# A decoder layer on one core: the input projection written out as one stream in TensorE's program order

## The chip, the cores and the metric

The kernel runs on one core of a Trainium2 chip. The metric is the device time of one execution in microseconds (us); the median of several executions counts. Beside the times there is one profiled execution, whose trace gives the start and the length of the instructions on each engine: PE (TensorE's matmuls), PEld (its weight loads), DVE (VectorE), ACT (ScalarE), POOL (GpSimd) and SP (SyncE, which issues most DMAs).

## What is computed

One layer (DEPTH is 1) over 2048 rows of 1024 numbers, all float32:

```python
h = rms_norm(x, mix_norm_pre)
z = h @ w_in                                   # 1024 -> 2560: q, k, v, xr, gr of 512 each
attn = dilated_attention(q, k, v)              # 8 heads of 64, three dilation patterns
xr = causal_depthwise_conv(xr, conv_w, conv_b) # four taps
rec = rg_lru(xr, ...) * gelu(gr)               # gates r and i, a linear recurrence over time
x = x + rms_norm(concat([attn, rec]) @ w_out, mix_norm_post)
x = x + rms_norm(squared_relu_mlp(rms_norm(x, mlp_norm_pre)), mlp_norm_post)
```

The gates are `sigmoid(xr @ w_r + b_r)` and `sigmoid(xr @ w_i + b_i)` in blocks of 64; the recurrence is `h[t] = a[t] * h[t-1] + u[t]` with `a = exp(-8 r softplus(-lambda))`.

## The kernel before

Every float32 product is made of three matmuls on a high and a low part of each operand, split with a cast on ACT and a subtraction on DVE or POOL. The sequence is worked in two halves of 1024 rows, each of two blocks `b` of 512 rows. For each half there come the input projection, the attention, the recurrent part, the output projection and the MLP. The attention of the second half is already mixed into the MLP of the first.

This study is about the first stage, which holds the input projection of both halves, the recurrent part of both halves and the attention of the first half. `w_in` is cut into 20 column tiles `ct` of 128: 0 to 3 are q, 4 to 7 k, 8 to 11 v, 12 to 15 xr, 16 to 19 gr. `Project.product` makes one tile for one block: 8 steps over `k` of three matmuls of 512 columns, 24 matmuls, into one PSUM bank named `z`. Two halves, two blocks and 20 tiles make 80 products. `load_w` loads a tile's weights and splits them (`wraw`, `wH`, `wL`); `load_x` loads a block of x transposed and splits it (`hH`, `hL`); `spread_norm` spreads the norm's factors over the partitions through a product with ones (`pbc`, `bc`).

`qkv(hf, pr)` makes q, k and v for a pair of heads and stores them in DRAM. `recurrent_block(hf, c, b)` makes an xr product, the four taps (`xc`, the first on POOL, three on DVE), the two gate matmuls `pr` and `pi`, some ten steps on ACT and DVE up to the scan, the gr product, the gelu (`ge`, its polynomial on POOL) and the output. `attention` has for each head two parts of kind A (scores `S`) and four of kind B (`SB`); each part has its scores, a mask and maximum on DVE, an exponential on ACT (`sm`), transposes on PE (`pT`), a split (`thA`, `tlA` or `thB`, `tlB`) and value products (`oA`, `oB`). `join` merges the two kinds.

The stage is called in the order of the strings `ORDER`, `BETWEEN` and `LATER` (q for `qkv`, r for `recurrent`, a for the attention of a pair, x for `load_x`), but the instructions do not stand in that order: a scheduler of the framework orders every engine's instructions of this stage. From the output projection on, PE's order is that of the code, and in the second half's attention ACT's, DVE's and SP's too: there `interleave` puts the attention's steps between steps of the MLP's second product.

## Time and profile before

| | us |
|---|---|
| median of 3 executions | 2320.88 (2314.49 to 2322.9) |
| profiled execution, its own time | 2311.64 |
| its span in the trace | 2309.9 |
| PE busy | 2184.8 (95%) |
| DVE busy | 1539.9 (67%) |
| ACT busy | 1231.3 (53%) |
| POOL busy | 465.9 (20%) |

The span is the time from the first to the last instruction; a little time lies around it. Matmuls are pipelined, so a PE that is shown busy may still run below its pace: how fast it runs is read from the distance between the starts of equal matmuls. The first matmul of the output projection (`m`) starts at 650.8 us; what lies before is the stage of the change.

### The profile page before, as it was taken

How to read it: one execution, taken by the hardware profiler on the slowest of the kernel's cores; microseconds unless marked ns; L12 is line 12 of the kernel's file. 1: busy time of each engine (PE TensorE's matmuls, PEld its weight loads, DVE VectorE, ACT ScalarE, POOL GpSimd, SP SyncE). 2: the span in 40 equal slices, each digit the busy share in tenths (PEclk: the TensorE clock that was granted, in tenths of full speed). 3: DMA queues.
4: the chain of work that ended last, by engine and by line, in shares of the span. 5: the costliest groups of instructions: out<-in, count | busy, mean ns of one | idle time of the engine just before them, and what ended most of it. 6: DMA issues, size and time to landing. Idle time of an engine off the chain costs nothing.

```text
span 2309.9 us, 30833 instructions
## 1 busy us (share of the span) xinstructions
PE 2184.8 (95%) x10264; PEld 1776.1 (77%) x10264; DVE 1539.9 (67%) x3060; ACT 1231.3 (53%) x2489; POOL 465.9 (20%) x549
## 2 busy tenths in 40 slices
PE   8989989889999899998999999889999999999998
PEld 6668778667788677786777787667878888788887
DVE  6757575887548877674667677767775656545556
ACT  7646464645334555453656666745454545563542
POOL 5543514563213201011001011113200000000003
PEclk9999999999999999999999999999999999999999
DMA  8364574645754586867777777768454433576665
GB/s 288 99 194 154 166 232 146 180 144 151 255 166 155 195 306 255 302 232 268 248 201 211 220 227 204 220 189 257 147 194 169 164 137 155 208 271 195 192 192 182
DMA packets 217553, 466.16 MB, mean 202 GB/s; under 512 B 22465, under 2 KB 77153, under 8 KB 211121
## 3 DMA queue, kind: packets, MB, share of 16 engines
q1 hardware_dynamic: 188624, 329.52, 45.7%
q0 software_dynamic: 28768, 134.66, 16.5%
q8 instruction: 81, 1.33, 0.2%
q14 instruction: 80, 0.65, 0.1%
HBM read 329.75 MB, written 151.13 MB: 208 GB/s over the span
## 4 chain that ended last, share of the span: by engine, by line
PE 59%; DVE 14%; DMA 9%; ACT 7%; issue 5%; POOL 1%; SPq 0%; DVEq 0%; ACTq 0%; POOLq 0%
PE o L1141 6%; PE o L1140 6%; PE o L1142 6%; PE za L1001 4%; PE za L1002 4%; PE za L1003 4%; PE z L198 3%; PE z L199 3%; PE z L200 3%; PE m L827 2%; PE m L825 2%; PE m L826 2%; PE zc L1001 2%; PE zc L1002 2%; PE zc L1003 2%
## 5 line engine op out<-in xcount | busy, mean ns | idle before, releaser
L198 PE MATMUL z<-hH,wH 128*128 128x512 f32 x640 | 263.6, 412 | 17.6 <-ACT wH L54 7.9
L199 PE MATMUL z<-hL,wH 128*128 128x512 f32 x640 | 259.1, 405 | 0.5 <-DVE hL L173 0.5
L200 PE MATMUL z<-hH,wL 128*128 128x512 f32 x640 | 257.9, 404 | 0.0
L198 PEld LDWEIGHTS z<-hH,wH 128*128 128x128 f32 x640 | 122.6, 192 | 51.2 <-ACT wH L54 8.8
L199 PEld LDWEIGHTS z<-hL,wH 128*128 128x128 f32 x640 | 122.3, 191 | 32.0 <-issue 5.1
L200 PEld LDWEIGHTS z<-hH,wL 128*128 128x128 f32 x640 | 122.5, 191 | 28.5 <-issue 3.4
L415 ACT ACTIVATE smB<-smB,negB 128x128 f32<-128x128 f32 (+3 forms) x128 | 71.4, 559 | 103.0 <-DVE negB L411 102.7
L55 POOL TENSOR_TENSOR wL<-wraw,wH 128x512 fp32r<-128x512 f32 x58 | 84.2, 1464 | 115.7 <-ACT wH L54 109.0
L1006 ACT ACTIVATE sq<-sq 128x512 f32<-128x512 f32 x93 | 58.8, 632 | 84.9 <-DVE sq L1010 84.9
L1066 POOL DMA_DIRECT2D sa<-sq x31 | 16.5, 533 | 402.4 <-ACT sq L1007 401.8
L415 ACT ACTIVATE sm<-sm,neg 128x256 f32<-128x256 f32 (+1 forms) x128 | 63.1, 494 | 55.7 <-DVE neg L411 55.2
L55 DVE TENSOR_TENSOR tlB<-pT_B,thB 128x384 fp32r<-128x384 f32 x96 | 57.4, 598 | 44.2 <-ACT thB L54 41.0
L1007 ACT ACTIVATE sq<-sq 128x512 f32<-128x512 f32 x124 | 76.6, 629 | 2.2
L54 ACT CAST wH<-wraw 128x512 fp32r<-128x512 f32 (+1 forms) x81 | 47.2, 612 | 49.5 <-PE z L199 31.7
L1174 POOL TENSOR_TENSOR y<-y,g4b 128x512 f32<-128x512 f32 x8 | 13.0, 1655 | 261.3 <-ACT junk_y L84 261.3
L1077 DVE TENSOR_TENSOR w2s<-w2s 128x512 f32<-128x512 f32 x64 | 44.1, 689 | 32.1 <-DMA w2s<-in_dram 31.2
L404 DVE CUSTOM_DVE_ANT_0 smB<-SB,mask_b 128x128 f32<-128x128 f32 (+3 forms) x128 | 59.5, 482 | 6.8 <-PE pT_B L377 4.2
L377 PE MATMUL pT_B<-ident,smB 128*128 128x128 f32 x320 | 52.7, 280 | 5.3 <-DVE nb L398 2.2
L54 ACT CAST thB<-pT_B 128x384 fp32r<-128x384 f32 x96 | 48.4, 506 | 16.3 <-PE oB L612 14.2
L55 DVE TENSOR_TENSOR tlA<-pT,thA 128x512 fp32r<-128x512 f32 (+1 forms) x64 | 42.5, 668 | 21.0 <-ACT thA L54 20.7
L1001 PE MATMUL za<-hHT,f_6H 128*128 128x512 f32 x128 | 50.6, 396 | 5.2 <-ACT sq L1040 5.1
L1002 PE MATMUL za<-hLT,f_5H 128*128 128x512 f32 x128 | 51.0, 399 | 4.4 <-DVE hLT L55 4.4
(568 smaller groups left out, 7105.7 us busy)
## 6 DMA issues: line engine op xcount, KB each, us to landing
sa<-as POOLq DMA_DIRECT2D x32, 1024.0 KB, 6.5
w1r<-in_dram SPq DMA_DIRECT2D x58, 512.0 KB, 3.8
sa<-sq POOLq DMA_DIRECT2D x31, 768.0 KB, 3.9
wraw<-in_dram SPq DMA_DIRECT2D x79, 256.0 KB, 3.5
w2s<-in_dram SPq DMA_DIRECT2D x16, 1024.0 KB, 7.5
sb<-w2s POOLq DMA_DIRECT2D x16, 1024.0 KB, 6.2
kh<-sk SPq DMA_DIRECT2D x24, 512.0 KB, 5.2
kl<-sk SPq DMA_DIRECT2D x24, 512.0 KB, 6.8
```

What stands on the lines that cost most here:

```text
L54: return (nc.scalar.copy(out=hi, in_=src), (lo_eng or nc.vector).tensor_tensor(out=lo, in0=src, in1=f32(hi), op=ALU.subtract))
L55: (lo_eng or nc.vector).tensor_tensor(out=lo, in0=src, in1=f32(hi), op=ALU.subtract))
L198: pe.matmul(z, hi[:, k, :], hh, start=(k == 0), stop=False)
L199: pe.matmul(z, hi[:, k, :], hl, start=False, stop=False)
L200: pe.matmul(z, lo[:, k, :], hh, start=False, stop=(k == KT - 1))
L415: s.activation(out=sm[:, c0:c0 + w], in_=sm[:, c0:c0 + w], func=AF.Exp, bias=neg[:, j:j + 1], accum_out=st[:, 1, u, cols[j]:cols[j] + 1])
L1001: pe.matmul(o, hi[:, k], bh[:, k], start=start and k == 0, stop=False, skip_group_check=True)
L1002: pe.matmul(o, hi[:, k], bl[:, k], start=False, stop=False, skip_group_check=True)
L1003: pe.matmul(o, lo[:, k], bh[:, k], start=False, stop=k == KH - 1, skip_group_check=True)
L1140: pe.matmul(o, ah[:, ts], bh, start=fresh and j == 0, stop=False, skip_group_check=True)
L1141: pe.matmul(o, ah[:, ts], bl, start=False, stop=False, skip_group_check=True)
L1142: pe.matmul(o, al[:, ts], bh, start=False, stop=j == NJ - 1, skip_group_check=True)
```

## The change

The stage keeps its arithmetic but gets a new frame. `product` becomes a generator that pauses after each of its 8 steps. `stream` runs all products in the order of the table `JOBS` (a token such as `0k3v3` is half 0 and the tiles k3 and v3 together, block by block), loads the weights of the next tile at each tile's first block, and does what follows a product: `stored` (q, k, v), `convolved` and `opened` (taps and gates), `gated` (gelu). What of that needs PE is put off by `after(n, ...)`: it is issued when n further steps of products have gone by. `begin` does the same by hand for the first eight products. PE's instructions of the whole stage are now in program order (`manual_schedule`); those of the other engines are still ordered by the scheduler. The first half's attention goes through `interleave`, which already served the second half's, with gaps of its own, and `join`'s last steps are spread too.

Three pieces of work change engine. The first tap goes from POOL to ACT, and so do from DVE the two small copies of the taps' tail and the square of `r`. The gelu's polynomial, three steps on POOL, becomes a square on ACT and one step on DVE. The copies of `w_out` and `w2` from DRAM to DRAM, which are issued on POOL's queue, came one with each call (`w_out`) and then eight with each call of `recurrent` for the second half (`w2`); now one or two come with each product, from the first stored q on.

```diff
+            if px:
+                made(j)
+                spread(j)
+            else:
+                self.after(4 + 3 * j, lambda j=j: made(j))
+                self.after(6 + 3 * j, lambda j=j: spread(j))
         self.bc[tb % NBH] = bcast
...
     def product(self, hf, ct, w, b, tag="P"):
+
         hi, lo = w
         pe = self.nc.tensor
         z = self.bank(tag, f"z{hf}_{ct}_{b}")
...
-        return z
-
-    def qkv(self, hf, pr):
+            yield z
+
+    def stored(self, kind, hf, pr, b, z):
...
+
+        self.after(4, turned)
...
+    def after(self, n, fn):
+
+        self.due.append([n, fn])
+
+    def passed(self):
+        for d in self.due:
+            d[0] -= 1
+        now = [d for d in self.due if d[0] <= 0]
+        self.due = [d for d in self.due if d[0] > 0]
+        for _, fn in now:
+            fn()
+
+    def stream(self, jobs, between):
+
+
+        first = {"q": 0, "k": 4, "v": 8, "x": 12, "g": 16}
+        jobs = [(int(t[0]), [(t[i], int(t[i + 1])) for i in range(1, len(t), 2)]) for t in jobs.split()]
+        tiles = [(hf, kind, i) for hf, ts in jobs for kind, i in ts]
+        loaded = {}
+
+        def load():
+            if tiles:
+                hf, kind, i = tiles.pop(0)
+                loaded[hf, kind, i] = self.load_w(hf, first[kind] + i)
+
+        load()
+        for hf, ts in jobs:
+            for b in range(NBH):
+                for kind, i in ts:
+                    if b == 0:
+                        load()
+                    between(hf, kind, i, b)
+                    for n, last in enumerate(self.product(hf, first[kind] + i, loaded[hf, kind, i], b)):
+                        self.passed()
+                        if n < KT - 1:
+                            yield
+                    if kind in "qkv":
+                        self.stored(kind, hf, i, b, last)
+                    elif kind == "x":
+                        self.convolved(hf, i, b, last, 10)
+                    else:
+                        self.gated(hf, i, b, last)
+                    yield
+        while self.due:
+            self.passed()
...
+    def begin(self, w, px):
...
+        for c in range(2):
+            product("x", c, 0, "B")
+            product("g", c, 0, "T")
+        self.after(5, first)
+        product("x", 0, 1, "P")
+        product("g", 0, 1, "P")
+        self.after(3, second)
+        product("x", 1, 1, "B")
+        self.gated(0, 0, 1, z["g", 0, 1], px)
+        product("g", 1, 1, "T")
+        followed(1, 1, 24)
+
...
-def interleave(units, rest):
+def interleave(units, rest, begin, gaps, pause=0):
...
-        turn[0]()
-        fill(2)
-        fill(2, ahead[0]())
-        if early:
-            loads[0](False)
-            if k % n == 3:
-                loads.pop(0)
-        turn[1]()
-        fill(2)
-        fill(1 if k + n >= len(todo) else 2 - k % 2, ahead[1]())
+
+        whole = k + 1 < len(todo) and len(todo[k + 1][1]) == 1
+        if pause:
+            then = ahead[0]()
+            fill(gaps[0], ahead[1]() if whole else then)
+            turn[0]()
+            fill(gaps[1])
+            if early:
+                loads[0](False)
+                if k % n == 3:
+                    loads.pop(0)
+            then = None if whole else ahead[1]()
+            fill(gaps[2], then)
+            if len(turn) > 1:
+                turn[1]()
+        else:
+            turn[0]()
+            fill(gaps[0])
+            fill(gaps[1], ahead[0]())
+            if early:
+                loads[0](False)
+                if k % n == 3:
+                    loads.pop(0)
+            turn[1]()
+            fill(gaps[2])
+        fill(gaps[3 + k % 2] if k + n < len(todo) else gaps[5], None if pause else ahead[1]())
         values()
         if ending:
             ends.append(ending())
+            fill(pause)
     while ends:
         fill(1)
 
...
+            def between(hf, kind, i, b):
+
+                if (hf, kind, i, b) in NEWX:
+                    n = NEWX[hf, kind, i, b]
+                    pj.load_x(n)
+                    pj.spread_norm(n)
+                if "pool" not in cst:
+                    return
+                with tc.issue_after(cst["pool"].ins):
+                    for dst, src in copies[:1 if len(copies) > 2 * NJ else 2]:
+                        nc.gpsimd.dma_start(out=dst, in_=src)
+                del copies[:1 if len(copies) > 2 * NJ else 2]
...
-            with sb("at0", "right") as pa:
-                attend = attention(tc, pa, lambda k, n: bank(place[k][0], n), cst, scr, 0, mask_a, mask_b, pa)
-                run(ORDER)
-            pg = per.enter_context(sb("g2", "right"))
-            sh = Shared(pg, bank)
-            run(BETWEEN)
-            lst.close()
-            wo = load_wo(0)
-            pj.lo = nc.vector
-            run(LATER)
+            with tc.manual_schedule(engines={mybir.EngineType.PE}):
+                steps = pj.stream(JOBS, between)
+                for _ in range(8 * AHEADJOBS):
+                    next(steps)
+                xst.close()
+                with sb("at0", "right") as pa:
+                    interleave(attention(tc, pa, lambda k, n: bank(place[k][0], n), cst, scr, 0, mask_a, mask_b, pa), steps,
+                               16, (1, 1, 1, 3, 4, 3), 10)
+                for _ in range(REST):
+                    next(steps)
+                pg = per.enter_context(sb("g2", "right"))
+                sh = Shared(pg, bank)
+                lst.close()
+                wo = load_wo(0)
+                pj.lo = nc.vector
+                for _ in steps:
+                    pass
...
-ORDER = "q00 r02 q01 a0 r03 q02 a1 q03 x2 x3 a2 q10 a3"
-BETWEEN = "r10 r11 r12 r13"
-LATER = "q11 q12 q13"
+
+
+JOBS = ("0q0 0k0 0v0 0x2 0g2 0q1 0k1 0v1 0q2 0k2 0v2 0x3 0q3 0g3 0k3v3 1x0q0 1g0 1k0 1x1 1v0 1g1 1x2 1g2 1x3 1g3 "
+        "1q1 1k1 1v1 1q2 1k2 1v2 1q3 1k3 1v3")
+
+NEWX = {(0, "k", 3, 1): 2, (1, "x", 0, 0): 3}
+AHEADJOBS = 10
+REST = 0
```

The taps, gates and gelu are now these:

```diff
         xr = p.tile([P, TB + 3], F32, tag="xr", bufs=1, name=f"xr{n}")
-        v.tensor_copy(out=xr[:, 0:3], in_=self.tail[:, c, :])
+        s.copy(out=xr[:, 0:3], in_=self.tail[:, c, :])
         v.tensor_tensor(out=in_time(xr[:, 3:TB + 3]), in0=by_residue(zx), in1=by_residue(self.bc[b]), op=ALU.mult)
-        v.tensor_copy(out=self.tail[:, c, :], in_=xr[:, TB:TB + 3])
+        s.copy(out=self.tail[:, c, :], in_=xr[:, TB:TB + 3])
         xc = p.tile([P, TB], F32, tag="xc", bufs=2 if p is self.pl else 1, name=f"xc{n}")
-        self.cst["pool"] = g.tensor_scalar(out=xc, in0=xr[:, 3:TB + 3], scalar1=self.cw[:, c, 3:4],
-                                           scalar2=vec["cb"][:, c:c + 1], op0=ALU.mult, op1=ALU.add)
+        s.activation(out=xc, in_=xr[:, 3:TB + 3], func=AF.Identity, scale=self.cw[:, c, 3:4],
+                     bias=self.vec["cb"][:, c:c + 1])
...
+        self.xc[c, b], self.open[hf, c, b] = xc, None
+        self.after(wait, lambda: self.opened(hf, c, b, p, px))
+
+    def opened(self, hf, c, b, p, px):
...
         pr = self.bank("X", f"pr{n}")
         pe.matmul(pr, self.bd["r"][:, c, :], xc, start=True, stop=True)
-        pi = self.bank("O" if px else "X", f"pi{n}")
-        pe.matmul(pi, self.bd["i"][:, c, :], xc, start=True, stop=True)
...
-        a2 = p.tile([P, TB], F32, tag="la", bufs=1, name=f"a2{n}")
-        v.tensor_tensor(out=a2, in0=r, in1=r, op=ALU.mult)
...
+        def rest():
+            pi = self.bank("O" if px else "X", f"pi{n}")
+            pe.matmul(pi, self.bd["i"][:, c, :], xc, start=True, stop=True)
...
+            a2 = p.tile([P, TB], F32, tag="la", bufs=1, name=f"a2{n}")
+            s.activation(out=a2, in_=r, func=AF.Square)
...
+            ends = self.open.pop((hf, c, b))
+            if ends:
+                ends()
+
+        if px:
+            rest()
+        else:
+            self.after(4, rest)
...
         ge = p.tile([P, TB], F32, tag="ge", bufs=1, name=f"ge{n}")
-        g.tensor_tensor(out=ge, in0=gr, in1=gr, op=ALU.mult)
-        g.tensor_scalar(out=ge, in0=ge, scalar1=0.044715, scalar2=1.0, op0=ALU.mult, op1=ALU.add)
-        g.tensor_tensor(out=ge, in0=ge, in1=gr, op=ALU.mult)
-        s.activation(out=ge, in_=ge, func=AF.Tanh, scale=SQ2PI)
+        s.activation(out=ge, in_=gr, func=AF.Square)
+        v.scalar_tensor_tensor(out=ge, in0=ge, scalar=1.0 / 0.044715, in1=gr, op0=ALU.add, op1=ALU.mult)
+        s.activation(out=ge, in_=ge, func=AF.Tanh, scale=SQ2PI * 0.044715)
...
+        def ends():
+            v.scalar_tensor_tensor(out=by_residue(ge), in0=by_residue(ge), scalar=0.5, in1=in_time(xc), op0=ALU.mult,
+                                   op1=ALU.mult)
+            nc.gpsimd.dma_start(out=scr_cols(self.scr["mix"][hf][4 + c], b), in_=ge)
+
+        if (hf, c, b) in self.open:
+            self.open[hf, c, b] = ends
+        else:
+            self.after(5, ends)
```

On PE, the first place is the attention's first head, kind A: `S` and `pT` are its scores and transposes (numbers: half, head, first block), `z0_15_0` and `z0_19_0` are products of half 0, `z0_5_0` too. Before:

```order
L377 MATMUL pT0_0_0_1_0_1695<-ident_60,sm0_0_4_1682 128x128 x4
L200 MATMUL z0_15_0_2118<-hH0_6_335,wL0_15_1597 128x512
L198 MATMUL z0_15_0_2118<-hH0_7_341,wH0_15_1596 128x512
L199 MATMUL z0_15_0_2118<-hL0_7_342,wH0_15_1596 128x512
L377 MATMUL pT0_0_0_1_1_1714<-ident_60,sm0_0_6_1703 128x128 x2
L200 MATMUL z0_15_0_2118<-hH0_7_341,wL0_15_1597 128x512
L198 MATMUL z0_19_0_2171<-hH0_0_290,wH0_19_2108 128x512
L377 MATMUL pT0_0_0_1_1_1714<-ident_60,sm0_0_6_1703 128x128 x2
L199 MATMUL z0_19_0_2171<-hL0_0_291,wH0_19_2108 128x512
```

Of the change:

```order
L476 MATMUL pT0_0_0_0_0_1544<-ident_60,sm0_0_0_1473 128x128 x3
L206 MATMUL z0_5_0_1494<-hH0_5_323,wH0_5_1362 128x512
L207 MATMUL z0_5_0_1494<-hL0_5_324,wH0_5_1362 128x512
L208 MATMUL z0_5_0_1494<-hH0_5_323,wL0_5_1363 128x512
L621 MATMUL S0_0_6_1554<-kh0_0_1386,qa0_0_1389 128x256
L621 MATMUL S0_0_6_1554<-kl0_0_1387,qa0_0_1389 128x256
L621 MATMUL S0_0_6_1554<-kh0_0_1386,qa0_0_1389 128x256
L621 MATMUL S0_0_6_1554<-kl0_0_1387,qa0_0_1389 128x256
L206 MATMUL z0_5_0_1494<-hH0_6_329,wH0_5_1362 128x512
L207 MATMUL z0_5_0_1494<-hL0_6_330,wH0_5_1362 128x512
L208 MATMUL z0_5_0_1494<-hH0_6_329,wL0_5_1363 128x512
L476 MATMUL pT0_0_0_0_1_1569<-ident_60,sm0_0_2_1504 128x128 x4
```

The transposes of two neighbouring score tiles stood about four matmuls apart and were cut in two by a product's matmul; now each set stands whole, a step or two of a product (three matmuls each) is placed between every two attention steps, and the scores of the next tile stand between the transposes of this one.

On POOL, the place is the start of the second half's recurrent part: `wL` are low parts of weights, `zl` those of q and k, `xc` is the first tap, `ge` the gelu, `sw2` the copies of `w2`. Before:

```order
L55 TENSOR_TENSOR wL1_16_4668<-wraw1_16_0_4669,wH1_16_4667 128x512
L55 TENSOR_TENSOR wL1_16_4668<-wraw1_16_1_4673,wH1_16_4667 128x512
L307 TENSOR_SCALAR xc1_0_0_4706<-xr1_0_0_4702,cw_222,vec_cb_224 128x512
L338 TENSOR_TENSOR ge1_0_0_4757<-gr1_0_0_4755 128x512
L339 TENSOR_SCALAR ge1_0_0_4757<-ge1_0_0_4757 128x512
L340 TENSOR_TENSOR ge1_0_0_4757<-ge1_0_0_4757,gr1_0_0_4755 128x512
L55 TENSOR_TENSOR wL1_13_4862<-wraw1_13_0_4863,wH1_13_4861 128x512
L307 TENSOR_SCALAR xc1_0_1_4794<-xr1_0_1_4790,cw_222,vec_cb_224 128x512
L1459 DMA sw20_169<-in_16_dram 128x512
L1459 DMA sw20_169<-in_16_dram 128x1024
L1459 DMA sw21_170<-in_16_dram 128x512
```

Of the change:

```order
L439 DMA smix1_103<-ge1_0_0_3858 128x512
L55 TENSOR_TENSOR wL1_13_3937<-wraw1_13_0_3938,wH1_13_3936 128x512
L55 TENSOR_TENSOR wL1_13_3937<-wraw1_13_1_3942,wH1_13_3936 128x512
L439 DMA smix1_103<-ge1_0_1_3930 128x512
L55 TENSOR_TENSOR zl1_k0_0_4015<-zn1_k0_0_4012,zh1_k0_0_4014 128x512
L55 TENSOR_TENSOR wL1_8_4115<-wraw1_8_0_4116,wH1_8_4114 128x512
L55 TENSOR_TENSOR wL1_8_4115<-wraw1_8_1_4120,wH1_8_4114 128x512
L55 TENSOR_TENSOR zl1_k0_1_4107<-zn1_k0_1_4104,zh1_k0_1_4106 128x512
L55 TENSOR_TENSOR wL1_17_4305<-wraw1_17_0_4306,wH1_17_4304 128x512
```

The first tap and the three gelu steps of each block are gone from POOL, and the copies of `w2` have moved up into the first half's products.

## Rows read from the trace of the kernel before

**Rows 1.** The page: span and busy time of each engine over the execution.
```profile
span 2309.9 us, 30833 instructions
PE 2184.8 (95%) x10264; PEld 1776.1 (77%) x10264; DVE 1539.9 (67%) x3060; ACT 1231.3 (53%) x2489; POOL 465.9 (20%) x549
```

**Rows 2.** Busy time by stretch; the stretches of this stage and the second half's attention.
```profile
core 0: us, PE busy (x) PEld busy (x) DVE busy (x) ACT busy (x) POOL busy (x), PEclk, DMA share, GB/s
0.00:40.00 40.00, 32.24 (x124) 23.77 (x125) 25.80 (x66) 28.08 (x48) 16.13 (x28) 1.00 0.88 303
40.00:130.00 90.00, 85.19 (x353) 65.11 (x352) 65.20 (x85) 55.99 (x80) 51.34 (x54) 0.98 0.53 157
130.00:320.00 190.00, 179.10 (x944) 147.25 (x942) 116.81 (x297) 100.18 (x241) 74.07 (x65) 0.98 0.56 171
320.00:400.00 80.00, 72.20 (x382) 60.47 (x382) 48.77 (x127) 38.62 (x99) 27.63 (x24) 0.94 0.61 183
400.00:560.00 160.00, 140.15 (x675) 108.30 (x675) 139.14 (x268) 97.25 (x195) 83.47 (x89) 0.95 0.53 161
560.00:650.00 90.00, 88.63 (x417) 71.98 (x416) 47.31 (x76) 30.26 (x56) 15.86 (x13) 1.00 0.69 211
0.00:650.00 650.00, 597.51 (x2887) 476.89 (x2888) 443.03 (x915) 350.40 (x716) 268.49 (x271) 0.97 0.59 182
1109.00:1529.00 420.00, 393.81 (x2158) 327.67 (x2157) 302.77 (x757) 270.25 (x609) 37.84 (x68) 1.00 0.71 208
```

**Rows 3.** Tiles of the stage: duration min/median/max, first and last start.
```profile
L198 PE MATMUL z<-hH,wH x640: 387/394/1414, 5.1 to 649.6; 128*128 128x512 f32 x160
```

**Rows 4.** PE's timeline: start, duration, instruction, idle time before it.
```profile
82.66 0.39 PE L200 MATMUL z<-hH,wL 128*128 128x512 f32 x1
...
90.96 0.40 PE L200 MATMUL z<-hH,wL 128*128 128x512 f32 x1
...
100.37 1.78 PE L313 MATMUL pr<-xc,bd_r 128*128 128x512 f32 x2 [3.41 <-DVE xc L310]
```

**Rows 5.** PE's timeline at 453 to 468 us.
```profile
453.09 0.39 PE L199 MATMUL z<-hL,wH 128*128 128x512 f32 x1
458.95 0.58 PE L553 MATMUL oA<-thA,va 128*128 128x256 f32 x1 [5.47 <-DVE state L332]
```

**Rows 6.** PE's timeline where the second half's attention starts.
```profile
1108.94 0.28 PE L529 MATMUL S<-kh,qa 128*128 128x256 f32 x1
```

**Rows 7.** DVE's groups between 400 and 560 us, shapes apart.
```profile
L310 DVE SCALAR_TENSOR_TENSOR xc<-xr,cw,xc 128x512 f32<-128x512 f32 x21 | 23.7, 1127 | 2.3 <-POOL xc L307 2.0
L331 DVE TENSOR_TENSOR_SCAN xc<-r,state,i 128x512 f32<-128x512 f32 x8 | 11.5, 1441 | 0.2
L343 DVE SCALAR_TENSOR_TENSOR ge<-ge,xc 128x512 f32<-128x512 f32 x7 | 9.0, 1282 | 0.1
L329 DVE SCALAR_TENSOR_TENSOR i<-i,xc 128x512 f32<-128x512 f32 x8 | 8.4, 1049 | 0.8 <-ACT i L320 0.8
...
L326 DVE TENSOR_TENSOR a<-r 128x512 f32<-128x512 f32 x7 | 5.8, 830 | 8.5 <-ACT r L324 8.5
L305 DVE COPY tail<-xr 128x3 f32<-128x3 f32 x7 | 5.1, 724 | 0.0
...
L303 DVE COPY xr<-tail 128x3 f32<-128x3 f32 x6 | 4.0, 664 | 0.1
```

**Rows 8.** The taps' tile `xc`: duration ns min/median/max.
```profile
L310 DVE SCALAR_TENSOR_TENSOR xc<-xr,cw,xc x48: 720/752/3589, 40.4 to 535.2; 128x512 f32<-128x512 f32 x48
...
L329 DVE SCALAR_TENSOR_TENSOR i<-i,xc x16: 679/692/2756, 50.8 to 552.7; 128x512 f32<-128x512 f32 x16
L331 DVE TENSOR_TENSOR_SCAN xc<-r,state,i x16: 1268/1283/2196, 73.5 to 558.1; 128x512 f32<-128x512 f32 x16
...
L343 DVE SCALAR_TENSOR_TENSOR ge<-ge,xc x16: 1060/1078/1895, 75.4 to 561.9; 128x512 f32<-128x512 f32 x16
```

**Rows 9.** POOL's groups in the stage, 0 to 650 us.
```profile
L340 POOL TENSOR_TENSOR ge<-ge,gr 128x512 f32<-128x512 f32 x16 | 23.3, 1453 | 1.0
L338 POOL TENSOR_TENSOR ge<-gr 128x512 f32<-128x512 f32 x16 | 19.3, 1205 | 24.5 <-DVE gr L335 17.1 <-DMA smix<-ge 7.3
...
L307 POOL TENSOR_SCALAR xc<-xr,cw,vec_cb 128x512 f32<-128x512 f32 x16 | 13.6, 851 | 32.9 <-DVE xr L304 32.5 <-DVE negB L411 0.2
L339 POOL TENSOR_SCALAR ge<-ge 128x512 f32<-128x512 f32 x16 | 13.4, 835 | 1.5
```

**Rows 10.** ACT's groups in the stage, 0 to 650 us.
```profile
L172 ACT ACTIVATE hH<-xr,g_sb 128x512 fp32r<-128x512 f32 x32 | 22.0, 718 | 16.2 <-DMA xr<-in_dram 14.3 <-DMA g_sb<-in_dram 1.9
L328 ACT ACT_TABLE_LOAD x16 | 20.5, 1283 | 0.3
...
L328 ACT ACTIVATE th<-th 128x512 f32<-128x512 f32 x16 | 10.1, 632 | 16.1 <-DVE th L327 16.0
...
L146 ACT ACTIVATION_READ_ACCUMULATOR xn<-xn 128x1 f32 x16 | 3.0, 188 | 0.0
```

**Rows 11.** Waits over the execution: total us, times, longest.
```profile
DVE tlB L55 <- ACT thB L54: 41.0, 44, 2.9
```

**Rows 12.** The copies of `w2` in DRAM.
```profile
L1459 POOL DMA_DIRECT2D sw<-in_dram x32: 521/523/569, 409.6 to 532.6; - x32
DMA to landing us min/median/max: 2.6/5.8/17.2
```

More of the change, by code (lines that the diff above doesn't have):

```diff
@@ new lines, in turned @@
+        def turned():
+            pt = self.bank("X", f"vt{n}")
+            for j in range(TB // P):
+                pe.transpose(pt[:, j * P:(j + 1) * P], zn[:, j * P:(j + 1) * P], self.cst["ident"])
+            ptv = pt.rearrange("p (n h c) -> p n h c", h=2, c=HD)
+            vs = self.pa.tile([P, TB // P, 2, 2, HD], F32R, tag="vst", bufs=1, name=f"vs{n}")
+            split(nc, vs[:, :, :, 0, :], vs[:, :, :, 1, :], ptv)
+            nc.sync.dma_start(out=f32(scr["v"][hf][pr][cs, :].rearrange("(n p) c -> p n c", p=P)),
+                              in_=f32(vs.rearrange("p n u a c -> p n (u a c)")))
@@ L287, in recurrent_consts, with product, followed, first @@
         v.memset(self.state, 0.0)
-    def recurrent(self, hf, cs, w=None, px=None):
-        w = w or {k + c: self.load_w(hf, k + c, px=px) for c in cs for k in (12, 16)}
-        for b in range(NBH):
-            for c in cs:
-                self.recurrent_block(hf, c, b, w[12 + c], w[16 + c], px)
-    def recurrent_block(self, hf, c, b, wx, wg, px):
-        nc, p, vec = self.nc, px if px and c % 2 else self.pl, self.vec
-        v, s, g, pe = nc.vector, nc.scalar, nc.gpsimd, nc.tensor
+    def begin(self, w, px):
+        z = {}
+        def product(k, c, b, tag):
+            for z[k, c, b] in self.product(0, (12 if k == "x" else 16) + c, w[(12 if k == "x" else 16) + c], b, tag):
+                self.passed()
+        def followed(c, b, wait):
+            self.convolved(0, c, b, z["x", c, b], wait, px)
+            self.gated(0, c, b, z["g", c, b], px)
+        def first():
+            self.spread_norm(0, px)
+            followed(0, 0, 9)
+            followed(1, 0, 20)
+        def second():
+            self.spread_norm(1, px)
+            self.convolved(0, 0, 1, z["x", 0, 1], 9, px)
+        for c in range(2):
[9 more added lines that the diff above has]
+        followed(1, 1, 24)
@@ L674, in weights @@
             ccs.append(cc)
-        amid = hf and pr < NP - 1
-        e = v if amid else g
+        amid = pr < NP - 1
+        e = v if hf and amid else g
         for b in range(NBH):
@@ L696, in join @@
             nc.gpsimd.dma_start(out=scr["mix"][hf][pr][:, cs], in_=na[:, cs])
-    def pair(pr):
-        todo, ending, _ = units(pr)
-        for scores, turn, values in todo:
-            if len(turn) == 2:
-                for f, t in zip(scores, turn):
-                    f()
-                    t()
-            else:
-                for f in scores + turn:
-                    f()
-            values()
-        for _ in ending():
-            pass
-    return units if hf else pair
+    return units
 SMB = (3, 4)
@@ L1309, in fill @@
                 then()
+        if not n and then:
+            then()
         if ends and next(ends[0], True):
@@ L1320, in interleave @@
     for _ in range(8):
[L1321 removed]
+        fill(begin // 8)
         loads[0](False)
```

194 lines of the change are left out of this document (74 added, 120 removed).

## The prediction

> **What bounds the kernel now.** The page says that PE is busy for 2184.8 of 2309.9 us [rows 1], but an average over stages hides where something can be won. So the next view is busy time by stretch [rows 2]. The change touches only what stands before the output projection, about 0 to 650 us: the last matmul of the input projection starts at 649.6 [rows 3]. PE is busy there for 597.5 us, so 52.5 are idle. Some of the busy time is slow as well: where the granted clock is 0.98, 0.94 or 0.95, the missing share of the stretch is lost. That makes 90 x 0.02 + 190 x 0.02 + 80 x 0.06 + 160 x 0.05 = 18.4 us. The stage thus holds 650 - 52.5 - 18.4 = 579.1 us of PE work at full clock. The loss of 70.9 us is the most that any order of the same matmuls can give back. Nothing behind the stage gets shorter.
>
> The loss is uneven. Taken per stretch, length less idle less slow clock gives the work: 32.2, 83.4, 175.3, 67.4, 132.2 and 88.6 us. The start loses 7.8 us while the DMA engines are at 0.88. The stretch 40 to 130 loses 6.6 us. The stretch 400 to 560, where the second half's recurrent part stands, loses 19.9 idle + 8.0 clock = 27.8 us, 21% of its work; DVE is busy there for 139.1 of 160 us, 87%. The last stretch, projection alone, loses 1.4 us, 1.5%. What ends the waits is seen on PE's timeline: at 96.6 us PE stands 3.41 us for the taps before the gate matmul `pr` [rows 4], and at 453.1 us it stands 5.47 us until DVE comes past the recurrence's `state`, although the next instruction is an attention product [rows 5]. So PE waits in its own order for links that go through DVE, POOL and ACT, and DVE's queue is the thickest of these.
>
> **The change, part by part.** The matmuls stay the same, so the 579.1 us stay. Their pace when nothing is late: 36 matmuls from 82.66 to 90.96 us [rows 4], 0.2306 us each, so a product of 24 takes 5.53 us. The order of the changed program has 20 of the 80 products ahead of the first attention scores, 43 between these and the last attention product, and 17 behind it. The last 17 are 94.1 us; the first 20 come to 110.7, with their gate matmuls about the 115.6 us of work of 0 to 130; 369.4 us are left for the middle. Of its 43 products, 20 belong to the first half (stretch A, 171.8 us of work) and 23 to the second (stretch B, 197.6), with the eight recurrent blocks of that half.
>
> What does the new order lose? The nearest relative in this trace is the attention of the second half, which starts at 1108.94 [rows 6] and is already written out by `interleave`: 393.8 of 420 us busy at clock 1.00, a loss of 26.2 us or 6.65% of the work, with DVE at 302.8, 72% [rows 2]. I take this rate for A: 11.4 us. B is thicker on DVE. The stretch 400 to 560 is its like, and the change alters DVE's work in it so: the two small copies go (5.1 + 4.0) and the square `a` (5.8) [rows 7]; a gelu step comes, 7 x 0.69 like `i` [rows 8], 4.8. DVE's steps there are also longer than their medians [rows 7, 8]: taps 21 x 0.375, scan 8 x 0.158, `ge` 7 x 0.204 and `i` 8 x 0.357, 13.4 us together. POOL drops 23.3 + 19.3 + 13.6 + 13.4 = 69.6 us of the stage's 268.5 [rows 9, 2], 4.35 us a block; eight blocks are 34.8 of the 83.5 us that POOL is busy in this stretch, 42%, so I count 42% of the 13.4 as relief, 5.6. DVE then has 139.1 - 9.1 - 5.8 + 4.8 - 5.6 = 123.4 us beside 132.2 of PE work. On the line through the two known points (72%, 6.65%) and (87%, 21%) this balances at a length of 152.5 us: DVE 81%, loss 15.3%. B has the same eight blocks beside 197.6 us of PE work, though beside attention parts throughout, so I take 11%, between 6.65 and 15.3: 21.7 us.
>
> What POOL's leaving does to DVE can be read from single steps: a tap takes 752 ns at the median and 3589 at most [rows 8]. The Trainium skill ("SBUF — State Buffer", section on SBUF's two separate sides) says that a VectorE instruction with two SBUF inputs and a GpSimd instruction that reads SBUF take one shared pair of ports as a lock and wait for each other whole. By that rule, what stays on POOL (the low parts of weights, q and k) locks DVE as before whenever they meet; if they meet as often, the relief of 5.6 us is nothing and B goes towards the 21% of today, which is the second rival below.
>
> The start keeps its 7.8 us, since the same loads stand there in the same order. The next stretch keeps 6.6: `begin` fixes PE's order but the taps still follow the norm. The tail runs like 560 to 650: 94.1 x 0.0155 = 1.5.
>
> The rest I put at nothing. ACT takes for each of 16 blocks two squares (0.63 like the activation at L328), a tap (0.72 like L172) and two small copies (0.19, like an accumulator read) [rows 10]: 2.4 us, 38 in all, and 350.4 [rows 2] become 388, 60% of 650, less than DVE's 68%. Were the copies 0.72 each, it would be 55 us more. Table loads of 1.28 us [rows 10] would matter, but both programs hold 50. The `w2` copies, issued from 409.6 to 532.6 us now [rows 12], move into the first half's products, where the DMA share is 0.56 [rows 2]; weights are loaded a tile, 11 us, ahead. A landing at its worst, 17.2 us [rows 12], would make a product wait some 6 us; behind it in PE's order all else waits. I allow 0 to 12 us for that, and 0 to 12.6 for the new rows of x at the turn of the halves, which is what 320 to 400 loses today; 8.6 of that are already in B's 11%.
>
> **Sum.** 579.1 + 7.8 + 6.6 + 11.4 + 21.7 + 1.5 = 628.1 us, 21.9 less than 650. The profiled execution would go from 2311.64 to 2289.7. It stands 9.2 us under the median shown, 2320.88, so for the median I forecast 2299.0.
>
> **Rivals.** *The stream runs clean* (0.18): the lags are long enough that the middle loses like the tail, 1.5%: 5.7 us. The stage is 579.1 + 15.9 + 5.7 = 600.7, the median 2271.6. For it speaks that each attention step now has a step or two of products before the next; against it that `interleave` loses 6.65% today with a lighter DVE.
>
> *DVE stays the pace-maker* (0.22): the order only moves PE's waits, and B loses 21% like 400 to 560: 41.5 us. The stage is 579.1 + 15.9 + 11.4 + 41.5 = 647.9, the median 2318.8: no change. For it speaks that DVE's work hardly falls and that its order is still the scheduler's, as at 453 us [rows 5].
>
> *Every joint of the attention stops PE* (0.14, slower). Before, a late transpose or value product could have a product of another tile pulled ahead of it; now PE stands. The half has 48 attention parts with two joints each, transposes after exponentials and value products after the low parts. If a joint costs what DVE waits for ACT at `tlB`, 41.0/44 = 0.93 us [rows 11], the middle loses 89 us and the stage is 684, the median 2355. It becomes slower by 0.5% when the joints cost (661.6 - 579.1 - 15.9) / 96 = 0.69 us each.
>
> **The numbers.** The forecast has 0.46, with a range of its own of 2286 to 2311. 0.5%, 11.6 us, is about what a measurement can tell from no change. All of the clean case and nearly all of the forecast are faster than that: 0.64. DVE's case is the same: 0.22. The joints: 0.14. The range goes from 2266, the clean case with a little less lost at the start, to 2324, past DVE's case by a late weight; beyond it lie most of the joints' case and little else.
>
> **What the profile will show.** If I am right, the first `m` starts near 628 us, the granted clock is at 0.98 or more in every stretch, the longest waits of PE in A are under 1 us, and B has DVE at about 80% and PE idle for some 10%. POOL's busy time falls by about 70 us and the taps' mean, now 1127 ns in the thick stretch [rows 7], falls below 0.95 us. I am wrong if PE waits for `wH` or `hH` by several us at a time (the loads), if transposes wait for `sm` throughout (the joints), or if the taps stay as long (no relief from POOL).

## The result, and the profile after

The changed kernel takes 2326.20 us (median of 15, 2316.21 to 2332.71), the kernel before 2317.06 (median of 15); the ratio is 1.0042 with a 95% interval of 1.0026 to 1.0058. It is slower, by 9.7 us: inside the half per cent that the prediction calls the same, and not the gain of 21.9 us that it forecast. The profiled execution of the change took 2326.59 us.

The page of the change, span and busy time, beside [rows 1]:

```profile
span 2324.7 us, 30774 instructions
PE 2191.8 (94%) x10264; PEld 1778.9 (77%) x10264; DVE 1510.7 (65%) x3022; ACT 1268.2 (55%) x2569; POOL 404.5 (17%) x491
```

DVE and POOL did get their relief, and PE got nothing. The first `m` starts at 650.8 us in both profiles. To see where the stage loses, it is cut where its work changes: up to the first scores `S`, from there to the last value product `oB`, and from there to the first `m`. Busy time by these stretches, first the kernel before, then the change (columns as in [rows 2]):

```profile
0.00:130.60 130.60, 118.03 (x478) 89.39 (x479) 91.60 (x150) 84.07 (x127) 68.06 (x82) 0.99 0.64 202
130.60:571.00 440.40, 401.85 (x2053) 324.81 (x2052) 312.48 (x704) 240.78 (x544) 185.16 (x178) 0.96 0.56 168
571.00:650.80 79.80, 78.43 (x366) 63.35 (x365) 38.96 (x62) 25.61 (x46) 15.27 (x12) 1.00 0.71 221
```

```profile
0.00:158.60 158.60, 135.59 (x528) 99.88 (x529) 96.52 (x156) 107.43 (x172) 56.13 (x77) 0.96 0.69 219
158.60:547.80 389.20, 363.10 (x1915) 295.41 (x1914) 270.34 (x650) 248.98 (x571) 129.92 (x120) 0.97 0.52 162
547.80:650.80 103.00, 99.83 (x452) 81.02 (x452) 46.78 (x73) 30.69 (x54) 20.36 (x17) 0.98 0.66 198
```

Loss is again length less busy time, plus length times the missing clock. Before: 13.9 us ahead of the scores, 56.2 in the middle, 1.4 in the tail. After: 29.4, 37.8 and 5.2. The middle gives back 18.4 us; the start takes 15.5 and the tail 3.8.

The start's loss is one chain, read backwards from PE. At 120.18 PE had issued its last matmul; it then stood 7.73 us. Three timelines of the change, PE, DVE and ACT:

```profile
120.18 0.40 PE L208 MATMUL z<-hH,wL 128*128 128x512 f32 x1
128.31 0.77 PE L206 MATMUL z<-hH,wH 128*128 128x512 f32 x1 [7.73 <-DVE xr L374]
```

```profile
109.14 0.69 DVE L221 TENSOR_TENSOR zn_v<-z,bc 128x512 f32<-128x512 f32 x1 [1.56 <-PE z L208]
126.50 0.69 DVE L55 TENSOR_TENSOR vs_v<-vt_v,vs_v 128x512 fp32r<-128x512 f32 x1 [16.67 <-ACT vs_v L54]
127.11 1.05 DVE L374 TENSOR_TENSOR xr<-z,bc 128x512 f32<-128x512 f32 x1
```

```profile
108.83 1.15 ACT L54 CAST wH<-wraw 128x512 fp32r<-128x512 f32 x2 [1.97 <-PE z L207]
125.89 0.58 ACT L54 CAST vs_v<-vt_v 128x512 fp32r<-128x512 f32 x1 [15.91 <-DMA sv<-vs_v]
```

ACT waits 15.91 us to write the second split of v, since its tile (tag `vst` in the code, `vs_v` in the rows) has one buffer and the first is still being stored. DVE's low part waits behind ACT, `xr` behind it on DVE's queue, and the product that needs the bank which `xr` reads is next in PE's order. The store is late for this reason, seen in the transfers of the change from 95 to 128 us (KB each, median us to landing) and in the landing time of its v stores at 90 to 131 us:

```profile
swo<-in_dram POOLq DMA_DIRECT2D x6, 512.0 KB, 8.3
sv<-vs_v SPq DMA_DIRECT2D x2, 512.0 KB, 10.7
sw<-in_dram POOLq DMA_DIRECT2D x2, 512.0 KB, 12.4
sw<-in_dram POOLq DMA_DIRECT2D x2, 256.0 KB, 12.9
```

```profile
DMA to landing us min/median/max: 3.3/10.7/18.1
```

Ten copies stand there, six of `w_out` and four of `w2`; before, the same stretch holds one, of `w_out`, and the one landing of a v store that its trace has there is 3.2 us. After the stop the matmuls stand some 0.43 us apart instead of 0.23; from 123 to 133 us the granted clock is 0.50, the lower of its two levels.

Behind the stage PE's order should not have changed, but at three places it did. `fill(pause)` with a pause of 0 issues no product, but it still advances the join by a step. In the second half's attention the join's products `pst` are thus issued ten matmuls earlier (six of the MLP's, four scores), and PE waits longer for DVE's `sa`. PE's waits there, 1100 to 1540 us (total, times, longest), before, where four joins fall into the stretch, and in the change, where three do:

```profile
PE pst L644 <- DVE sa L637: 3.3, 4, 0.9
PE pst L736 <- DVE sa L729: 4.3, 3, 1.4
```

### The profile page after: what moved, and what is told of

Same layout as the page of the kernel before. It is cut to its first block, busy times and chain, and to the rows that moved or that the text cites. A ratio compares the mean times of both kernels' runs of the same rounds, so it can differ in the third digit from the quotient of the medians.

```text
span 2324.7 us, 30774 instructions
## 1 busy us (share of the span) xinstructions
PE 2191.8 (94%) x10264; PEld 1778.9 (77%) x10264; DVE 1510.7 (65%) x3022; ACT 1268.2 (55%) x2569; POOL 404.5 (17%) x491
## 4 chain that ended last, share of the span: by engine, by line
PE 49%; DVE 12%; DMA 8%; ACT 7%; issue 6%; POOL 1%; SPq 0%; DVEq 0%; ACTq 0%; POOLq 0%
PE o L1220 6%; PE o L1221 5%; PE o L1219 5%; PE za L1080 4%; PE za L1081 4%; PE za L1082 4%; PE m L906 2%; PE m L904 2%; PE m L905 2%; PE zc L1080 2%; PE zc L1081 2%; PE zc L1082 2%; DMA w2s<-in_dram 2%; PE z L206 1%; PE z L207 1%
## 5 line engine op out<-in xcount | busy, mean ns | idle before, releaser
L206 PE MATMUL z<-hH,wH 128*128 128x512 f32 x640 | 272.8, 426 | 14.8 <-DVE xr L374 7.7
L704 PE MATMUL oB<-tlB,vb 128*128 128x256 f32 x192 | 47.0, 294 | 12.6 <-DVE tlB L55 10.7
```

The source lines that it names most:

```text
L206: pe.matmul(z, hi[:, k, :], hh, start=(k == 0), stop=False)
```

## The experiments

Ratios are to the kernel before, timed on the same chip; 0.001 is 2.3 us. Where two runs are compared, the difference of their ratios is meant; with intervals of some 0.0015 to either side, such a difference is uncertain by about 0.002, 5 us.

**The kernel before again** (`e1_before`, no edit).

> The kernel before, unchanged, profiled a second time, because its first profile (2311.64 us) lies 5.4 us under its median of 2317.06. If the two programs really need the same time for the first stage, the first matmul of the output projection starts here between 645 and 656 us, near the 650.8 us that both profiles show. If the first profile was a lucky one in that stage, it starts at 656 us or later, and the change did win some 5 us there.

One execution, 2319.24 us, first `m` at 647.8. The stage of the kernel before is thus not longer than its first profile said, and the change won nothing there. Its time behind the stage was: 2309.9 - 650.8 = 1659.1 us in the first profile, 2317.5 - 647.8 = 1669.7 here, and 2324.7 - 650.8 = 1673.9 in the change. Two profiles of one kernel differ by 10 us in that part, so small losses are read below from ratios and not from one trace.

**Without the extra step of the join** (`e2_join`).

```diff
             ends.append(ending())
-            fill(pause)
+            if pause:
+                fill(pause)
```

> The change, with the one extra step taken away that the new line in interleave gives to the join in the second half's attention (a fill of 0 still advances the join). Theory 1, the extra step costs: the join's products pst then stand six matmuls later on TensorE as before the change, the wait in front of them falls from about 1.6 to 1.0 us and the transposes behind stand where they stood; at about 1.4 us for each of three pairs of heads, 4 us go, and the ratio to before falls from 1.004 to about 1.0025. Theory 2, what is lost behind the first stage is DMA weather and not the step: the ratio stays at 1.004.

1.0024 (1.0009 to 1.0040), 0.0018 or 4.2 us less than the change, as theory 1 said, though the two intervals overlap, so that this run alone doesn't show it. PE's waits for `pst` in the same stretch of this run, 0.8 us a join instead of 1.4:

```profile
PE pst L736 <- DVE sa L729: 2.4, 3, 0.8
```

**Copies held back to the second half** (`e3_late`).

```diff
-                if "pool" not in cst:
+                if "pool" not in cst or hf == 0:
                     return
```

> The change, with the copies of w_out and w2 held back until the products of the second half. Theory 1, the burst of copies: at 80 to 140 us the copies fill the DMA engines, the store of the first v tile takes 18.1 us instead of 4.7, ACT stands 15.9 us for its buffer, DVE 16.7 and TensorE 7.7, and the clock falls for 10 us; without them that wait is gone, 7.7 + 5 = 12.7 us, the output projection starts at about 638 us and the ratio is about 0.999. Theory 2, TensorE's fixed order stalls there by itself: a wait of 5 us or more stays between 120 and 130 us, the stage ends near 650 and the ratio stays at 1.004. Theory 3, the copies cost the same wherever they are: the wait moves to 400 to 560 us, and the ratio stays at 1.004 too.

0.9993 (0.9980 to 1.0006): 11.4 us less than the change, theory 1. Without the copies ACT goes on 8.8 us after the first v store was issued, instead of 18.2 us, and its wait falls from 15.91 to 9.82 us (the store is issued 2.8 us later on SP's queue, behind loads of q and k). PE's stop of 7.73 us is gone; one of 3.06 us, until DVE has written `zn_v`, ends at 114 us. (In the kernel before the store lands after 3.2 us, not after the 4.7 of the expectation.) ACT's wait, and the stretches, cut in the same way:

```profile
119.19 0.59 ACT L54 CAST vs_v<-vt_v 128x512 fp32r<-128x512 f32 x1 [9.82 <-DMA sv<-vs_v]
```

```profile
0.00:151.40 151.40, 134.66 (x528) 101.17 (x529) 95.13 (x156) 107.27 (x172) 49.59 (x63) 0.98 0.59 190
151.40:540.00 388.60, 363.45 (x1915) 295.66 (x1915) 270.77 (x650) 248.14 (x572) 133.93 (x131) 0.98 0.55 176
540.00:642.10 102.10, 99.97 (x452) 80.98 (x452) 45.91 (x73) 30.70 (x54) 21.87 (x19) 0.98 0.68 208
```

The start loses 19.8 us instead of 29.4; the middle, to which the copies went, loses 32.9, not more than 37.8. Theory 3 is out.

**The moves alone, in the order before** (`e4_moves`). Tap, tail copies, square of `r` and gelu as in the change, nothing else.

> The kernel before with one part of the change alone: first tap and gelu off GpSimd, tail copies and the square of r to ACT; order and copies as before. Theory 1 (the prediction's term): the relief of DVE is about 5.6 + 9 + 5.8 - 4.8 = 15.6 us of its 139 us in the thick stretch, of which TensorE gets back 5 to 10 us; ratio 0.996 to 0.998. Theory 2, DVE's length next to GpSimd does not matter for TensorE: 0.999 to 1.001. Theory 3, ACT becomes the link that is late: slower than 1.002.

1.0050 (1.0033 to 1.0067), at first sight theory 3. But the longest stop of PE is this one, behind a row of 32 copies that were issued from 373.9 to 410.1 us (before: 409.6 to 532.6, [rows 12]):

```profile
424.92 1.22 PE L313 MATMUL pr<-xc,bd_r 128*128 128x512 f32 x1 [12.28 <-ACT i L320]
```

Among the late links is a load of weights: one that was issued after 374 us lands after 20.0 us, and ACT waits 11.15 us for a load of weights:

```profile
418.80 0.62 ACT L54 CAST wH<-wraw 128x512 fp32r<-128x512 f32 x1 [11.15 <-DMA wraw<-in_dram]
```

The copies of `w2` were tied to the first tap (`cst["pool"]`), which holds them in place on POOL's queue. With the tap on ACT all 32 follow the latest low part of q or k instead, and POOL issues them as soon as that is done. In the change they follow the latest low part too, but come one or two with each product.

**The moves alone, copies paced** (`e6_moves_paced`): as the run before, and

```diff
-        nc.gpsimd.dma_start(out=scr_cols(self.scr["mix"][hf][4 + c], b), in_=ge)
+        self.cst["pool"] = nc.gpsimd.dma_start(out=scr_cols(self.scr["mix"][hf][4 + c], b), in_=ge)
```

> The moves to ACT alone in the kernel before, again, but with the copies of w2 kept paced: they follow the store of each recurrent block on GpSimd's queue, since the first tap that they followed is no longer an instruction of that queue (without it, 32 copies were issued in 36 us from 374 us on, and TensorE then stood 12.3 us). Theory 1, the prediction's relief of DVE: 5 to 10 us, ratio 0.996 to 0.998. Theory 2, the relief gives TensorE nothing and the burst was the whole loss of the run before (1.005): 0.999 to 1.001. Theory 3, ACT becomes late with the added work: above 1.002, with TensorE's longest waits on ACT's r and i.

0.9964 (0.9949 to 0.9980), 8.3 us faster than before: theory 1, without any of the new order. This run and the one before it differ only in where the copies stand, and that is 0.0086, 20 us. The middle stretch of this run:

```profile
132.60:525.60 393.00, 371.40 (x1951) 304.63 (x1950) 268.16 (x654) 245.66 (x573) 130.40 (x125) 0.97 0.56 171
```

A loss of 33.4 us instead of 56.2, so the gain that the change shows in its middle is had here in the scheduler's order.

**Both repairs** (`e7_both`: the edits of `e2_join` and `e3_late`).

> The change with both repairs: no extra step of the join in the second half, copies held back to the second half. If the two losses are independent, the ratios add: 1.0042 - 0.0018 - 0.0049 = 0.9975, some 6 us faster than before. Rival: the time won in the first stage or in the attention is eaten by what follows: 0.9993, as with late copies alone.

0.9967 (0.9951 to 0.9983): near the sum of the two repairs, and level with the moves alone. Beside late copies alone it is 0.0026 or 6.0 us less, a second sign that the extra step of the join costs 4 to 6 us. Losses by stretch: 20.5, 27.6 and 4.0.

**Both repairs, tap and gelu back on POOL** (`e8_poolback`).

> Both repairs, and the gelu's polynomial and the first tap back on GpSimd: the new order without these moves. Theory 1, the moves relieve DVE next to GpSimd as the prediction counted (5.6 us in the second half, with more from the first): this is 5 to 10 us slower than with both repairs, ratio 1.000 to 1.002, and the taps' median or mean is longer. Theory 2, the moves are worth nothing to TensorE: within 0.001 of the run with both repairs. Theory 3, ACT's added work is what is late: this is faster than that run, below 0.996.

1.0091 (1.0068 to 1.0113), far beyond theory 1's 1.002. Part of the reason is the experiment's own. The held-back copies now stand ahead of the taps on POOL's queue, here before PE's stop of 11.70 us at 460.85:

```profile
454.78 0.53 POOL L1552 DMA_DIRECT2D sw<-in_dram  x1 [0.71 <-DMA sw<-in_dram]
457.01 0.52 POOL L1552 DMA_DIRECT2D sw<-in_dram  x1 [1.70 <-DMA sw<-in_dram]
457.57 0.77 POOL L377 TENSOR_SCALAR xc<-xr,cw,vec_cb 128x512 f32<-128x512 f32 x1
```

So it doesn't price the moves; the run with the order alone, below, does it better.

**A longer lag for the transposes of v** (`e9_lag6`): both repairs, and

```diff
-        self.after(4, turned)
+        self.after(6, turned)
```

> Both repairs, and the transposes of v put off by six steps of products instead of four. With late copies TensorE stood 1.3, 3.1, 2.0 and 2.1 us before such transposes until DVE had scaled the product. Theory 1, a lag that is too short in a fixed order: the four waits fall below 0.5 us each and 6 to 8 us go, ratio 0.003 below the run with both repairs. Theory 2, DVE is late there whatever stands next: the waits move to the next instruction of TensorE that needs DVE, and the ratio stays within 0.001.

0.9977 (0.9960 to 0.9994), within 0.001 of both repairs. Of the waits before these transposes only one of over 0.7 us is left (3.35 at 114 us), but others have come: 5.78 us before `pbc` and 5.24 before `pi`, both until DVE's `vs_v` is done. Theory 2: what is late stays late.

**Copies paced in the new order** (`e10_paced`): no extra step; one copy of `w_out` for every third product of the first half, four of `w2` behind the store of each block of the second half. **The same with all moves undone** (`e11_order`; `w2`'s copies behind the first tap): the new order alone. **The same as e10 with PE's order in `begin` left to the scheduler** (`e12_begin`):

```diff
-            with tc.manual_schedule(engines={mybir.EngineType.PE}):
-                pj.begin(w, px)
+            pj.begin(w, px)
```

> The change without the extra step of the join, and with the copies paced as before the change: w_out one for every third product of the first half, w2 four behind the store of each of the second half's recurrent blocks. Theory 1, copies amid the stream cost by their place and bursts: TensorE's waits for vs and va at 300 to 350 us and the 9.8 us of ACT at 110 us stay (they are there with late copies too), the stage ends within 5 us of 638, ratio 0.995 to 0.998. Theory 2, the order as such, once its copies are paced like those of the run with the moves alone (0.9964), is better than the scheduler's: below 0.994. Theory 3, pacing is worse than holding back: above 0.999.

> The same, with all moves undone: first tap and gelu's polynomial on GpSimd, tail copies and the square of r on DVE; w2 copies four behind each first tap. This is the new order alone. Theory 1, order and moves are independent and the order is worth nothing: ratio 0.999 to 1.002, as the kernel before, and 8 us over the run with paced copies. Theory 2, the fixed order needs the moves (each link through GpSimd that is late stops TensorE, which cannot go round it): above 1.004, 15 us or more over that run; part of what the run with both repairs and GpSimd's work showed (1.009) was then not the copies ahead of the taps. Theory 3, the order is worth the 16 us that the prediction's sum gave it without the relief: 0.993 to 0.995.

> Paced copies, no extra step, moves kept, but TensorE's instructions of the first eight products (begin) ordered by the scheduler as before the change. Theory 1, begin's fixed order costs what 40 to 130 us lose more than before the change (13 us instead of 7 to 8): that stretch loses below 9 us again, the first scores start near 147 us and the ratio falls by 0.002 under the run with paced copies. Theory 2, the wait there is DVE's and not the order's: TensorE waits as long in another place, and the ratio stays within 0.001.

Paced: 0.9977 (0.9961 to 0.9992), theory 1 in its ratio; the stage ended at 647.0 in that profile, later than expected. The order alone: 1.0032 (1.0015 to 1.0049), 7.4 us slower than before; it lies between theories 1 and 2. The moves, with the copies' place behind the stores that goes with them, are worth 12.7 us in this order, against 8.3 in the other; the difference is within the errors. Stretches of the order alone:

```profile
0.00:150.30 150.30, 134.21 (x528) 101.04 (x529) 100.94 (x167) 91.50 (x138) 78.92 (x90) 0.98 0.62 202
150.30:556.70 406.40, 372.58 (x1916) 302.26 (x1914) 294.21 (x670) 227.84 (x522) 178.84 (x171) 0.95 0.53 166
556.70:661.30 104.60, 100.04 (x453) 81.00 (x452) 49.92 (x73) 32.37 (x56) 21.76 (x18) 0.98 0.66 195
```

Losses of 19.1, 54.1 and 6.7: the middle loses what it lost before the change (56.2). `begin` without its fixed order: 1.0019 (1.0004 to 1.0034), 10 us slower than with it, the opposite of theory 1. From 40 to 130 us it loses 18.8 us (11.6 idle, clock 0.92), with the fixed order 10.2. So within the new code that part of the order is a gain; the kernel before loses 6.6 us there.

**Which of the moves** (`e13_gelu_tap`: tap and gelu off POOL, copies paced by the store; `e14_small`: only tail copies and the square of `r` from DVE to ACT; `e15_place`: no move, only the copies behind the store).

> The kernel before with only the moves off GpSimd: first tap to ACT, gelu's polynomial to ACT and DVE; tail copies and the square of r stay on DVE; copies of w2 paced by the store of each block. Theory 1, GpSimd's steps make DVE's steps beside them long, and that is the relief: most of the 8 us that all moves gave (0.9964), so 0.996 to 0.998, with the taps' mean between 400 and 560 us near 870 ns and the tail copies near 0.2 us instead of 0.7. Theory 2, the relief is the work taken from DVE (the prediction's larger part, 14.9 us of its time): 0.999 to 1.001.

> The kernel before with only the small steps moved from DVE to ACT: tail copies and the square of r; first tap and gelu stay on GpSimd, and so do the copies' places. Theory 1 (GpSimd's leaving is the relief): 0.999 to 1.001, the taps' mean stays above 1050 ns. Theory 2 (the work taken from DVE is the relief): 0.996 to 0.998.

> The kernel before with one thing changed: the copies of w2 follow the store of each recurrent block instead of its first tap, as in the runs with the moves; nothing moved off GpSimd. Theory 1, the relief comes from tap and gelu leaving GpSimd: 0.999 to 1.001. Theory 2, part of the 0.995 was the copies' new place: 0.996 to 0.998.

Tap and gelu: 0.9952 (0.9937 to 0.9968, from five executions), 11.1 us faster than before and the lowest ratio of all, though its interval overlaps that of all the moves. The small steps: 0.9993 (0.9980 to 1.0005), nothing clear of the noise. The copies' place: 0.9983 (0.9967 to 0.9998), some 4 us. So the place is worth about 4 us, with an error of 3 to 4, and what tap and gelu add by leaving POOL about 7, with an error of 5. Theory 1 fits best, with part of theory 2's place effect. The middle in the single profiles, with tap and gelu off POOL, with the small steps alone and with the place alone:

```profile
128.10:518.60 390.50, 368.14 (x1945) 300.88 (x1944) 274.69 (x680) 236.24 (x541) 130.46 (x125) 0.98 0.56 171
150.90:541.60 390.70, 359.75 (x1894) 293.00 (x1893) 273.28 (x638) 230.16 (x546) 166.79 (x165) 0.97 0.56 172
130.60:532.20 401.60, 371.64 (x1942) 302.68 (x1942) 285.15 (x672) 228.27 (x525) 171.29 (x167) 0.97 0.55 167
```

These are losses of 30.2, 42.7 and 42.0 us. The second lies 13.5 under the 56.2 of before although its ratio shows no gain, so the middle of one profile is no price either. One expectation failed: with tap and gelu gone, the tail copies still took 0.68 us, and those back into `xr` 0.33. The taps between 400 and 560 us, with tap and gelu off POOL and then with only the small steps moved, beside [rows 7]:

```profile
L310 DVE SCALAR_TENSOR_TENSOR xc<-xr,cw,xc 128x512 f32<-128x512 f32 x21 | 16.0, 760 | 2.2 <-ACT xc L307 2.1
```

```profile
L310 DVE SCALAR_TENSOR_TENSOR xc<-xr,cw,xc 128x512 f32<-128x512 f32 x20 | 28.6, 1430 | 2.3 <-POOL xc L307 2.0
```

1127 ns before, 760 without POOL's steps, 1430 without DVE's small ones. Such a mean rests on a few very long taps, and it does not follow the time: it is 955 with the copies' place alone, and 1035 in the change and 1109 with paced copies, both without tap and gelu on POOL. Of the 14.9 us taken from DVE between 400 and 560 us, 4.9 came back in the taps; DVE's busy time there still fell from 139.1 to 129.2 us.

## Why the prediction was wrong

**The start was to keep 7.8 + 6.6 = 14.4 us.** This is the largest step that failed. It lost 29.4: 6.2 up to 40 us, 20.4 instead of 6.6 from 40 to 130, and 2.8 up to the first scores. With late or paced copies and in the order alone the start still loses 17.5 to 20.5 us, though its first scores start some 20 us later than before, so a little of that belongs to the middle.

**The copies were put at nothing.** The prediction named those of `w2` only, but those of `w_out` moved up too, and six of the ten in front of the stop are theirs. All of them together cost 11.4 us where the change puts them, near the top of the 0 to 12 us that were allowed. The prediction looked for the harm at the weights; here it came through the store of v, with one buffer, and through three queues behind it. A landing as long stood in the rows: 17.2 us for a copy [rows 12], 18.1 here for the store. The diff shows the place, one or two with each product: all 40 are issued from 80.2 to 237.1 us, and from 98.8 to 532.6 before.

**The middle was sized nearly rightly, with some luck.** Stretches A and B were put at 11.4 + 21.7 = 33.1 us of loss; the change shows 37.8, and 27.6 and 32.9 in two runs with late copies. Ahead of the scores stand 129.2 us of work and not 115.6, so the 33.1 us were meant for more work than the 351.4 us that the middle holds. B begins with the 961st matmul of the products, so that each part can be cut out. A and B of the change, then of the order alone:

```profile
158.60:335.90 177.30, 166.86 (x896) 138.49 (x895) 106.64 (x283) 96.51 (x240) 65.97 (x69) 0.96 0.67 211
335.90:547.80 211.90, 196.24 (x1020) 156.92 (x1019) 163.70 (x367) 152.47 (x332) 63.94 (x51) 0.98 0.39 121
```

```profile
150.30:326.20 175.90, 167.91 (x897) 139.78 (x896) 111.96 (x289) 93.02 (x231) 63.90 (x56) 0.96 0.57 166
326.20:556.70 230.50, 204.66 (x1021) 162.47 (x1019) 182.25 (x381) 134.82 (x291) 114.94 (x115) 0.94 0.51 166
```

A loses 17.5 us in the change and B 19.9; in the order alone 15.0 and 39.7. So B came out as forecast only with the moves, and without them it loses 21% of its work, as the rival "DVE stays the pace-maker" has it. The order by itself gained nothing in the middle (54.1 us, 56.2 before), and the moves alone, with paced copies in the scheduler's order, lose no more there (33.4) than the change. Within the moves the step that failed is the split: most of the relief was counted as work taken from DVE (9.1 + 5.8), and POOL's leaving as 5.6 us, "42% of the 13.4". The runs show the reverse: the small steps alone gave nothing clear of the noise (0.9993), tap and gelu off POOL some 7 us.

**Behind the stage nothing was to change.** That was read from the stage's borders, not from PE's order behind them. The extra step of the join cost 4 to 6 us by two pairs of runs. **The tail** was put at 1.5 us and lost 5.2; why is not shown.

Together: 15.0 for the start, 4.7 for the middle and 3.7 for the tail bring the sum of 628.1 to 651.5, beside 650.8 measured.

**The rivals.** The time came out near "DVE stays the pace-maker" (2318.8), but not for its reason: it had B lose 21%, and in the change B loses 10%; from 400 to 560 us PE is busy for 151.37 of 160 us. The joints did not cost 0.69 us each: all idle time of the middle is 389.2 - 363.1 = 26.1 us, 0.27 for each of 96. Of the signs named, POOL's busy time did fall, by 62.1 us (268.49 to 206.41 in 0 to 650 us, against about 70 forecast), and the taps' mean fell to 1035 ns, not below 0.95 us.

**DVE beside POOL** is the step in which row and rule could have been weighed better. In the run with only the small steps moved, the longest tap takes 5.72 us. DVE's row, and POOL's rows at the same time:

```profile
443.89 5.72 DVE L310 SCALAR_TENSOR_TENSOR xc<-xr,cw,xc 128x512 f32<-128x512 f32 x1
```

```profile
444.13 2.50 POOL L55 TENSOR_TENSOR wL<-wraw,wH 128x512 fp32r<-128x512 f32 x2
446.59 1.25 POOL L689 TENSOR_TENSOR na<-na,co 128x512 f32<-128x512 f32 x1
447.81 1.25 POOL L340 TENSOR_TENSOR ge<-ge,gr 128x512 f32<-128x512 f32 x1
449.03 1.71 POOL L692 TENSOR_TENSOR nb<-nb,co 128x512 f32<-128x512 f32 x1
```

The tap stands through four POOL steps in a row (the first line holds two) and ends 0.6 us after the fourth, where POOL begins a fifth. The Trainium skill ("SBUF — State Buffer", section "SBUF: two separate sides") says that such a pair of instructions shares one pair of ports as an exclusive lock, held for a whole instruction; the trace agrees, and shows the hold over several instructions, which the page does not state. In the run with the copies' place alone, a DVE copy of three columns, 0.17 us at the median, stands through six POOL steps, with one DMA issue among them:

```profile
455.16 7.70 DVE L303 COPY xr<-tail 128x3 f32<-128x3 f32 x1
```

So what a step taken off POOL gives back depends on the row of POOL steps in which it stands, and a share of a mean excess, the 42%, does not tell it.

**What stays open.** Tap and gelu off POOL leave DVE's steps beside POOL shorter, and they also take POOL's queue out of the links that PE waits for; no run parts the two. Why the scheduler's order is as good as the written one in the middle was not found out by a run; the runs show that it is so with the moves (33.4 beside 27.6 to 39.5) and without them (56.2 beside 54.1).

## What to carry to other kernels

When an instruction changes engine, look for what was ordered by it: here a row of DMA issues was tied to the first tap, and in the moves alone 32 copies in a burst cost 20 us, more than the 8.3 that the moves gave. A transfer that nobody waits for is not free next to a store with one buffer, since the wait can climb, as here, through ACT and DVE to an engine that runs in a fixed order. Before a gain is given to a new order, run the engine moves that come with it alone, in the old order; and compare the instruction order behind the changed stage as well, for a shared helper carries the edit there.

## What was not expected of the hardware

A VectorE tap of some 0.75 us took 5.72 us beside four GpSimd steps in a row, and a copy of 0.17 us took 7.70 beside six. And taking 14.9 us of small steps from VectorE's busiest stretch gave nothing clear of the noise (0.9993).
